# Down products of the first FFN block by Strassen's scheme, for the second to fifth group of features

## The chip, the cores and the metric

The kernel runs on one core of one Trainium2 chip. The metric is the device time of one execution in microseconds (us). Engines are called as in the profile: PE is TensorE's matmul, PEld its weight load, DVE VectorE, ACT ScalarE, POOL GpSimd, SP SyncE, which issues the DMAs.

## The reference, cut to what matters

One layer over 2112 tokens (2048 of a prompt, 64 of a running stream), float32, model width 1024. The change lies in the last part, the SwiGLU FFN with 22 x 128 = 2816 hidden features:

```python
D_FF = -(-8 * D_MODEL // (3 * 256)) * 256
...
    x = x + jnp.concatenate([o_delta, o_pool], axis=-1) @ w_out
    h = rmsnorm(x, norm2_w)
    x = x + (jax.nn.silu(h @ w_gate) * (h @ w_up)) @ w_down
...
    y_prompt = rmsnorm(hp, normf_w)
```

## The kernel before, in words

The mixer (projection, gated delta rule, pooling, output projection) fills the first 940 us and is not touched. The FFN then runs over three blocks `b` of 704 tokens, each cut into two halves of 352 columns. All activations lie with features on the 128 partitions and tokens along the free dimension.

Every product is taken in three matmuls on split operands: an operand is rounded on ACT (the high part), and DVE subtracts that from the original (the low part); high x high, high x low and low x high are added in PSUM. "A split" below is this pair, one cast on ACT and one subtraction on DVE.

`gate_up(b, f)` makes one feature tile `f` of 128 features (0 to 21). It joins gate and up, two halves of the inner dimension and two halves of the tokens into a 2 x 2 product of blocks, by the Strassen-Winograd scheme: seven products of 12 matmuls (`px`, `py`, `pz` in the trace), 84 for a feature. Its weights are seven matrices: 11, 22 and 12 are raw parts, S1 to S4 are sums that POOL forms. In block 0 they are all formed and split here (four loads, four POOL operations `wrS`, seven splits `ws` and `wsS`), and S1 to S4 are stored in DRAM split; blocks 1 and 2 load those four back and split only three. The hidden value is `raw` (`hr` in the trace), 128 x 704.

The down product adds groups of features into eight output tiles `ys` (`y`), which stay in SBUF. The groups are FGROUPS = 4, 4, 4, 4, 2, 4 features, `gi` 0 to 5; the prediction calls them group one to six. There are two forms.

`down` (plain): for each of eight output tiles a weight tile is loaded, split (`wsd`) and multiplied; each half of each tile has its own PSUM sum (`d`), which DVE adds into `y`. The hidden features are split half by half into the tiles `h3`.

`down_strassen`: pairs of features and pairs of output tiles are again a 2 x 2 product of blocks. `prep_down` loads two raw tiles (`wrdt`, `wrdl`), POOL forms four combinations (`wrda`, `wrdb`), and four tiles are split (`wsd11`, `wsdS3`, `wsdS2`, `wsd22`). `factors` makes seven matrices of a pair of features: four combinations on POOL (`q` and `hr`), seven splits (`hq`, `h7`). Seven products go to three PSUM sums (`dx`, `dy`, `dz`), of which DVE takes 28 adds into `y` for a group of four.

In block 0 all six groups are plain (`SDOWN = (1, 2)` names the blocks that use the scheme), and the six-slot ring `h3t` holds the split features. In blocks 1 and 2 the groups go by the scheme, but for the very last one. `h3t`, the pairs made by `factors` and the plain pairs `two` share the tag `op`, which has two buffers: a pair's tile comes free when the down that reads it is done.

The list `order` puts `gate_up` of all features in a row and each group's down behind the first feature of the next group; for `gi` 0 it is one feature later (`LATER = 1`):

```python
order += [("dn", b, gi) for gi, (f0, G) in enumerate(groups) if f == min(f0 + G + LATER * (gi == 0), NF - 1)]
```

From it comes `plan`, the order in which weights are prepared, up to `AHEAD` = 3 entries before use. The raw tiles have four buffers and three (`wraw`, `wraw2`), the split ones four and four (`wsp`, `wsp2`); one feature takes seven split tiles, one step of a scheme down four. The helper `Machine` records all operations and writes each engine's instructions in an order of its own, by cost rules and ranks (`issue`, `pick`); PSUM evictions get a higher rank (`hurry`). Because it writes them all, every instruction has one line in the profile (L280), and groups are told apart by tile names. `stats2(1)`, which prepares block 1's input (`xd`, `xt`), runs in block 0 beside the first two groups; the queues are static, so each engine works strictly in the written order.

Of the kernel before, what the change touches and what calls it, by code (L numbers as in the profile page):

```python
# [25 lines left out]
NF = 22  # L26
# [18 lines left out]
SUBS2 = ((0, N2), (N2, N2))  # L45
FGROUPS = (4, 4, 4, 4, 2, 4)

SDOWN = (1, 2)
LASTPOOLS = {3: ((0,), (1,), (2, 3))}

FW = ("11", "S1", "S2", "12", "S3", "S4", "22")
# [310 lines left out]
def hybrid_kernel(ctx, tc, a, o):  # L362
# [11 lines left out]
    def mm(out, lhsT, rhs, start, stop, **kw):  # L374
        nc.tensor.matmul(out, lhsT, rhs, start=start, stop=stop, **kw)
        n = 1
        for d in out.shape[1:]:
            n *= d
        cost(n, rhs.dtype)
# [39 lines left out]
    def pump():  # L419
        for c in list(chains):  # L420
            if c.runnable() and c.at <= clock["pe"]:
                c.step()
# [80 lines left out]
    groups, f0 = [], 0  # L503
# [4 lines left out]
    def halves(b, gi):  # L508

        return ((0,), (1,)) if (b, gi) == (NB2 - 1, len(groups) - 1) else ((0, 1),)  # L510

    def plain(b, gi):
        return b not in SDOWN or len(halves(b, gi)) > 1

    order = []
    for b in range(NB2):
        for f in range(NF):
            order.append(("gu", b, f))
            order += [("dn", b, gi) for gi, (f0, G) in enumerate(groups) if f == min(f0 + G + LATER * (gi == 0), NF - 1)]
    for op in order:  # L520
        if op[0] == "gu":
            plan.append(("gu", op[2]))
        else:
            plan += [("dn", m, *groups[op[2]]) for m in range(KT)] * len(halves(*op[1:])) if plain(*op[1:]) else [
                ("ds", m, *groups[op[2]]) for m in range(KT // 2 * groups[op[2]][1] // 4)]
# [131 lines left out]
    def weights(*key):  # L657
        weights_ahead()
        k, hl = ready.pop(0)
        assert k == key, (k, key)  # L660
        return hl
# [21 lines left out]
    def split(dst, sl, src):  # L683
        nc.scalar.copy(dst[:, 0, sl], src)
        tt(dst[:, 1, sl], src, dst[:, 0, sl].bitcast(F32), ALU.subtract)
# [742 lines left out]
    def load_h(b, names):  # L1428
        for nm in names:
            for k in range(4):  # L1430
                t = hq[nm][k]
                if "pool" in wq:
                    raw = wq["pool"].tile([P, N2], F32, tag="t", name=f"xh{nm}{k}_{b}", bufs=TB)
                else:
                    raw = wpool.tile([P, 512], F32, tag="xs", name=f"xh{nm}{k}_{b}", bufs=XBUFS["xs"])[:, :N2]
                nc.sync.dma_start(out=raw, in_=hpd[b, FH.index(nm), k])
                nc.scalar.copy(t[:, 0], raw)
                (nc.gpsimd if b and k in HPOOL else nc.vector).tensor_tensor(
                    out=t[:, 1], in0=raw, in1=t[:, 0].bitcast(F32), op=ALU.subtract)
                yield LAT_LOAD  # L1440
# [80 lines left out]
    def tmp(nm):  # L1521
        return f2.tile([P, N2], F32, tag="t", name=nm, bufs=TB)

    def hurry(what, *args):

        machine.boost = HURRY
        what(*args)
        machine.boost = 0

    def gate_up(b, f):  # L1530
        w = weights("gu", f)
        tag = f"{b}_{f}"
        raw = f2.tile([P, 2, N2], F32, tag="hr", name=f"hr{tag}", bufs=3)

        def add(ps, nw, nh, first=False):

            for i, t in enumerate(hq[nh]):
                ks = slice(i * P, (i + 1) * P)
                for q, (wi, ai) in enumerate(((0, 0), (0, 1), (1, 0))):
                    mm(ps, w[nw][:, wi, ks], t[:, ai, :], start=first and i == q == 0, stop=i == 3 and q == 2,  # L1540
                       skip_group_check=not first)
                pump()

        def sigmoid(e, x):
            act(e, x, AF.Exp, scale=-1.0)
            act(e, e, AF.Ln, bias=onec)
            act(e, e, AF.Exp, scale=-1.0)

        def finish(i, g, u):
            e = raw[:, i]  # L1550
            tt(e, e, g, ALU.mult)
            tt(e, e, u, ALU.mult)
            if b not in SDOWN:
                split(h3t[f % 6], slice(i * N2, (i + 1) * N2), e)


        x, y, z = (psg(f"p{i}_{tag}")[:, :N2] for i in "xyz")
        add(x, "11", "11", True)
        hurry(nc.scalar.copy, g1 := tmp(f"g1_{tag}"), x)
        add(y, "S1", "T1", True)  # L1560
        hurry(nc.scalar.copy, u2 := tmp(f"u2_{tag}"), y)
        add(x, "S2", "T2")
        hurry(nc.scalar.copy, g2 := tmp(f"g2_{tag}"), x)
        add(z, "12", "21", True)
        hurry(tt, g1, z, g1, ALU.add)
        sigmoid(raw[:, 0], g1)
        add(x, "S3", "T3")
        hurry(tt, u2, x, u2, ALU.add)
        add(y, "S4", "22")
        hurry(tt, g2, y, g2, ALU.add)  # L1570
        sigmoid(raw[:, 1], g2)
        finish(1, g2, u2)
        add(x, "22", "T4")
        finish(0, g1, x)
        return raw if b in SDOWN else h3t[f % 6]

    def down(b, gi, h3, ys, which, done):
        f0, G = groups[gi]
# [9 lines left out]
    def factors(b, f, u, v):  # L1588

        t = opool.tile([P, 13, N2], F32R, tag="op", name=f"hq{b}_{f}", bufs=2)  # L1590
        low = f2.tile([P, N2], F32R, tag="h7", name=f"h7{b}_{f}", bufs=2)
        t = {nm: (t[:, 2 * i], t[:, 2 * i + 1] if i < 6 else low) for i, nm in enumerate(FH)}

        def split(nm, x):
            hi, lo = t[nm]
            nc.scalar.copy(hi, x)
            tt(lo, x, hi.bitcast(F32), ALU.subtract)

        gt = (nc.vector if f == NF - 1 else nc.gpsimd).tensor_tensor
        t3, t2, t4 = (tmp(f"q{i}{b}_{f}") for i in (3, 2, 4))  # L1600
        for nm, x in (("11", u[:, 0]), ("21", v[:, 0]), ("22", v[:, 1])):
            split(nm, x)
        gt(out=t3, in0=v[:, 1], in1=u[:, 1], op=ALU.subtract)
        gt(out=u[:, 1], in0=u[:, 1], in1=u[:, 0], op=ALU.subtract)
        gt(out=t2, in0=v[:, 1], in1=u[:, 1], op=ALU.subtract)
        gt(out=t4, in0=v[:, 0], in1=t2, op=ALU.subtract)
        for nm, x in (("T1", u[:, 1]), ("T2", t2), ("T3", t3), ("T4", t4)):
            split(nm, x)
        return t
# [23 lines left out]
    six = [opool.tile([P, 3, 2, TB2], F32R, tag="op", name=f"h3_{i}", bufs=2) for i in range(2)]  # L1633
    h3t = [six[i // 3][:, i % 3] for i in range(6)]
    h3, ys = {}, {}

    def between(b):

        if b >= 0:
            yield from final_norm(b, ys.pop(b))  # L1640
        ys[b + 1] = new_y(b + 1)
        if b + 2 < NB2:
            yield from stats2(b + 2, f2, "t", TB)

    for op in order:
        b = op[1]
        if op[0] == "gu":
            f = op[2]
            if f == 0:
                fill.finish()  # L1650
            if op == ("gu", 0, 2):
                nxt = Chain(between(-1))
            h3[f] = gate_up(b, f)
            if b in SDOWN:
                gi = max(g for g, (f0, G) in enumerate(groups) if f0 <= f)
                if plain(b, gi):
                    if f == groups[gi][0] or f == groups[gi][0] + 2:
                        two = opool.tile([P, 2, 2, TB2], F32R, tag="op", name=f"h3l{f}", bufs=2)
                    for i in range(2):
                        split(two[:, f % 2], slice(i * N2, (i + 1) * N2), h3[f][:, i])  # L1660
                    h3[f] = two[:, f % 2]
                elif f % 2:
                    machine.boost = HURRY if f == NF - 1 else 0
                    h3[f] = factors(b, f, h3.pop(f - 1), h3[f])
                    machine.boost = 0
            if f == NF - 1 and b + 1 < NB2:
                nxt.finish()
                fill = Chain(load_h(b + 1, FH))
        else:
            f0, G = groups[op[2]]  # L1670
            while b not in ys:
                nxt.step()
            hs = [h3.pop(f0 + i) for i in range(G) if f0 + i in h3]
            if not plain(b, op[2]):
                down_strassen(b, op[2], hs, ys[b])
            for which in halves(b, op[2]) if plain(b, op[2]) else ():
                done = []
                if which != (0, 1):
                    Chain(last_norm(b, ys[b], *which, done))
                down(b, op[2], hs, ys[b], which, done)  # L1680
            if op[2] == len(groups) - 1 and b + 1 < NB2:
                nxt = Chain(between(b))
# [24 lines left out]
LATER = 1  # L1707
# [125 lines left out]
```

## Time and profile before

| | |
|---|---|
| three runs, median (lowest to highest) | 2320.13 us (2318.85 to 2321.16) |
| the profiled execution, own time | 2319.95 us |
| its span, first to last instruction | 2318.1 us |
| busy: PE, DVE, ACT, POOL | 99%, 73%, 58%, 36% |
| granted TensorE clock, mean | 0.999 |
| FFN block 0, by PE's rows | 940 to 1407 us |

The busy shares are averages over stages. How the engines stand to each other in block 0 is read from the windows by cycle, one cycle being four gate/up features and one down. An engine's busy time in a window counts overlapping instructions once, while the mean of a group is the duration of each.

### The profile page before, as it was taken

The numbers are of one execution on the slowest core, as the hardware profiler recorded it, in microseconds if no ns is written. First come the engines' busy times: TensorE is split into PE (matmuls) and PEld (weight loads), VectorE is DVE, ScalarE is ACT, GpSimd is POOL, SyncE is SP. The second block draws the span as 40 slices with busy tenths as digits, with TensorE's granted clock in tenths as the row PEclk, the third lists the DMA queues.
The fourth block names the chain that finished last, engine by engine and source line by source line (L and its number), as shares of the span: only waits on it lengthen the run. The fifth ranks groups of instructions, "written<-read, shape, count | busy, mean of one in ns | idle before, by whom it ended". The sixth has DMA issues, their size and how long they took to land.

```text
span 2318.1 us, 41343 instructions
## 1 busy us (share of the span) xinstructions
PE 2290.5 (99%) x14614; PEld 2143.5 (92%) x14614; DVE 1685.2 (73%) x3085; ACT 1352.2 (58%) x3004; POOL 834.4 (36%) x943
## 2 busy tenths in 40 slices
PE   8999999999999999999999999999999999999998
PEld 8898898878777878999999999999999999999998
DVE  8988755673677786787657675877877878767776
ACT  6887855683768864565445465554454574454444
POOL 4424222440234350554412144643331654331312
PEclk9999999999999999999999999999999999999999
DMA  8755375545465568867645377768645586455463
GB/s 294 255 179 177 140 259 198 186 147 199 164 209 172 157 207 283 301 240 261 220 157 192 136 243 230 244 214 277 195 138 191 175 299 216 149 189 187 149 198 104
DMA packets 218751, 471.34 MB, mean 203 GB/s; under 512 B 27056, under 2 KB 85424, under 8 KB 218544
## 3 DMA queue, kind: packets, MB, share of 16 engines
q1 hardware_dynamic: 218544, 468.71, 60.0%
q8 instruction: 115, 1.88, 0.3%
q14 instruction: 92, 0.75, 0.1%
HBM read 354.81 MB, written 113.80 MB: 202 GB/s over the span
## 4 chain that ended last, share of the span: by engine, by line
PE 88%; DVE 6%; ACT 3%; DMA 1%; issue 1%; POOL 0%; SPq 0%; POOLq 0%; DVEq 0%; ACTq 0%
PE px L280 21%; PE pp L280 16%; PE pz L280 13%; PE py L280 10%; PE d L280 8%; PE dx L280 6%; PE dy L280 3%; PE pk_p L280 2%; PE pt_p L280 2%; PE dz L280 2%; PE gr_p L280 1%; DVE y L280 1%; PE py_p L280 1%; ACT E L280 1%; DVE Yqk L280 1%
## 5 line engine op out<-in xcount | busy, mean ns | idle before, releaser
L280 PE MATMUL pp<-h,wsp 128*128 128x512 f32 (+1 forms) x2480 | 558.3, 366 | 10.1 <-DVE wsp L280 9.3
L280 PEld LDWEIGHTS pp<-h,wsp 128*128 128x128 f32 x2480 | 400.6, 190 | 56.3 <-ACT wsp L280 8.7
L280 ACT CAST ws<-wr 128x512 fp32r<-128x512 f32 x198 | 122.0, 618 | 197.8 <-PE px L280 55.8
L280 DVE TENSOR_TENSOR ws<-wr,ws 128x512 fp32r<-128x512 f32 x198 | 167.0, 845 | 49.8 <-ACT ws L280 45.7
L280 PE MATMUL d<-h,wsd 128*128 128x352 f32 x1056 | 170.1, 322 | 0.0
L280 PEld LDWEIGHTS d<-h,wsd 128*128 128x128 f32 x1056 | 168.8, 188 | 0.0
L280 PE MATMUL pz<-op,wsp 128*128 128x288 f32 (+1 forms) x768 | 160.6, 352 | 0.0
L280 ACT ACTIVATE hr<-g 128x352 f32<-128x352 f32 x132 | 65.7, 498 | 135.6 <-DVE g L280 135.2
L280 PE MATMUL px<-hA,ws 128*128 128x352 f32 x792 | 143.7, 322 | 0.0
L280 PE MATMUL py<-hB,wsS 128*128 128x352 f32 x792 | 142.6, 322 | 0.0
L280 PE MATMUL pz<-hB,ws 128*128 128x352 f32 x792 | 142.1, 322 | 0.0
L280 POOL TENSOR_TENSOR wrS<-wr,wrS 128x512 f32<-128x512 f32 x44 | 63.1, 1434 | 215.5 <-DMA wrS<-in_wu_dram 117.4
L280 PE MATMUL py<-hA,wsS 128*128 128x352 f32 x792 | 140.4, 322 | 0.0
L280 ACT CAST TV_p<-pt_p 128x512 f16<-128x512 f32 x192 | 111.1, 586 | 47.9 <-PE pt_p L280 46.7
L280 PE MATMUL px<-hA,wsS 128*128 128x352 f32 x792 | 138.2, 322 | 0.5 <-ACT g L280 0.5
L280 PE MATMUL px<-hBT,ws 128*128 128x352 f32 x792 | 138.2, 323 | 0.2 <-DVE u L280 0.2
L280 PE MATMUL px<-hBT,wsS 128*128 128x352 f32 x792 | 137.7, 322 | 0.0
L280 PEld LDWEIGHTS pz<-op,wsp 128*128 128x128 f32 x768 | 121.2, 188 | 12.3
L280 PEld LDWEIGHTS px<-hA,wsS 128*128 128x128 f32 x792 | 128.7, 188 | 1.2 <-ACT g L280 1.1
L280 PEld LDWEIGHTS px<-hA,ws 128*128 128x128 f32 x792 | 129.8, 188 | 0.1
L280 PEld LDWEIGHTS py<-hB,wsS 128*128 128x128 f32 x792 | 129.6, 188 | 0.0
L280 PEld LDWEIGHTS pz<-hB,ws 128*128 128x128 f32 x792 | 129.5, 188 | 0.0
(689 smaller groups left out, 5589.4 us busy)
## 6 DMA issues: line engine op xcount, KB each, us to landing
wsS<-gS SPq DMA_DIRECT2D x176, 512.0 KB, 4.5
wsp<-wnd SPq DMA_DIRECT2D x126, 512.0 KB, 3.3
gS<-wsS SPq DMA_DIRECT2D x88, 512.0 KB, 4.4
wr<-in_wg_dram SPq DMA_DIRECT2D x132, 256.0 KB, 3.1
wnd<-wsp SPq DMA_DIRECT2D x42, 512.0 KB, 5.0
xd<-x2d SPq DMA_DIRECT2D x96, 176.0 KB, 3.3
wr<-in_wu_dram SPq DMA_DIRECT2D x66, 256.0 KB, 3.5
wrd<-in_wd_dram SPq DMA_DIRECT2D x56, 256.0 KB, 3.3
```

The costliest lines, as they stand in the source:

```text
L280: getattr(getattr(self.nc, op.eng), name)(*args, **kw)
```

## The change

`STR0 = (1, 2, 3, 4)` takes the place of `SDOWN`: in block 0 the groups two to five use `down_strassen` and `factors`; group one stays plain with the ring `h3t`, and group six is plain, with its features split into `two` as in the last group of block 2. `LATE0 = (1, 2)`: in block 0 the downs of groups two and three stand one feature later in `order`.

```diff
-SDOWN = (1, 2)
+STR0 = (1, 2, 3, 4)
+LATE0 = (1, 2)
...
     def plain(b, gi):
-        return b not in SDOWN or len(halves(b, gi)) > 1
+        return (b == 0 and gi not in STR0) or len(halves(b, gi)) > 1
...
-            order += [("dn", b, gi) for gi, (f0, G) in enumerate(groups) if f == min(f0 + G + LATER * (gi == 0), NF - 1)]
+            order += [("dn", b, gi) for gi, (f0, G) in enumerate(groups) if f == min(f0 + G + LATER * (gi == 0 or b == 0 and gi in LATE0), NF - 1)]
...
     def gate_up(b, f):
...
+        gi = max(g for g, (f0, G) in enumerate(groups) if f0 <= f)
+        six = b == 0 and gi < min(STR0)
...
-            if b not in SDOWN:
+            if six:
                 split(h3t[f % 6], slice(i * N2, (i + 1) * N2), e)
...
-        return raw if b in SDOWN else h3t[f % 6]
+        return h3t[f % 6] if six else raw
...
-            if b in SDOWN:
-                gi = max(g for g, (f0, G) in enumerate(groups) if f0 <= f)
+            gi = max(g for g, (f0, G) in enumerate(groups) if f0 <= f)
+            if b or gi >= min(STR0):
                 if plain(b, gi):
```

All engines' orders are the same up to feature 5 of block 0. On PE, before, group two's plain down (`d0_1_...`: block 0, `gi` 1, output tile, half) starts in the eighth feature (`px_0_8`, `py_0_8`):

```order
L280 MATMUL py_0_8_3223<-hB22_2908,wsS4_141_3190 128x352 x2
L280 MATMUL px_0_8_3222<-hBT3_2907,wsS3_141_3189 128x352 x12
L280 MATMUL py_0_8_3223<-hB22_2908,wsS4_141_3190 128x352 x10
L280 MATMUL d0_1_0_0_3230<-h3_1_2967,wsd_142_3199 128x352 x3
L280 MATMUL px_0_8_3222<-hBT4_2909,ws22_141_3191 128x352 x12
L280 MATMUL d0_1_0_0_3230<-h3_1_2967,wsd_142_3199 128x352 x3
L280 MATMUL d0_1_0_0_3230<-h3_0_2966,wsd_142_3199 128x352 x6
```

On PE, in the changed kernel, the same group's products (`dx0_1_0`, `dy0_1_0`, `dz0_1_0`: first pair of output tiles) start in feature 9 and read the pairs of features 4, 5 and 6, 7 (`hq0_5`, `hq0_7`):

```order
L281 MATMUL px_0_9_3271<-hBT3_2907,wsS3_142_3214 128x352 x12
L281 MATMUL py_0_9_3272<-hB22_2908,wsS4_142_3215 128x352 x6
L281 MATMUL dx0_1_0_3290<-hq0_5_3107,wsd11_143_3231 128x352 x3
L281 MATMUL dx0_1_0_3290<-hq0_7_3242,wsd11_143_3231 128x352 x3
L281 MATMUL px_0_9_3271<-hBT4_2909,ws22_142_3216 128x352 x12
L281 MATMUL dy0_1_0_3291<-hq0_5_3107,wsdS3_143_3232 128x352 x3
L281 MATMUL dy0_1_0_3291<-hq0_7_3242,wsdS3_143_3232 128x352 x3
L281 MATMUL dz0_1_0_3292<-hq0_5_3107,wsd11_143_3231 128x352 x3
L281 MATMUL dz0_1_0_3292<-hq0_7_3242,wsd11_143_3231 128x352 x3
L281 MATMUL dx0_1_0_3290<-hq0_5_3107,wsdS2_143_3233 128x352 x3
```

The plain sums, 12 matmuls for each half of an output tile, have become short runs of six on three sums, and the down has moved behind feature 9.

On DVE, before, around the last add of group two (`y7` from `d0_1_7`); 150 and 151 are the weights of features 9 and 10:

```order
L280 TENSOR_TENSOR wsS1_151_3272<-wrS1_151_3265,wsS1_151_3272 128x512
L280 TENSOR_TENSOR y7_0_3037<-y7_0_3037,d0_1_7_0_3294 128x352
L280 TENSOR_TENSOR y7_0_3037<-y7_0_3037,d0_1_7_1_3295 128x352
L280 TENSOR_TENSOR ws22_150_3261<-wr22_150_3250,ws22_150_3261 128x512
L280 TENSOR_TENSOR ws11_151_3271<-wr11_151_3264,ws11_151_3271 128x512
L280 TENSOR_TENSOR ws12_151_3274<-wr12_151_3267,ws12_151_3274 128x512
L280 TENSOR_TENSOR wsS2_151_3273<-wrS2_151_3269,wsS2_151_3273 128x512
L280 TENSOR_TENSOR g1_0_9_3314<-pz_0_9_3313,g1_0_9_3314 128x352
```

On DVE, in the changed kernel, around the last add of the same group; 147 is the weights of feature 10, the next one on PE, and `hq0_9`, `h70_9` are the factors of features 8 and 9:

```order
L281 TENSOR_TENSOR ws12_147_3303<-wr12_147_3296,ws12_147_3303 128x512
L281 TENSOR_TENSOR ws22_147_3306<-wr22_147_3295,ws22_147_3306 128x512
L281 TENSOR_TENSOR y7_0_3037<-y7_0_3037,dx0_1_3_3341 128x352
L281 TENSOR_TENSOR hq0_9_3277<-hr0_8_3255,hq0_9_3277 128x352
L281 TENSOR_TENSOR hq0_9_3277<-hr0_9_3270,hq0_9_3277 128x352 x2
L281 TENSOR_TENSOR hq0_9_3277<-hr0_8_3255,hq0_9_3277 128x352
L281 TENSOR_TENSOR hq0_9_3277<-q20_9_3280,hq0_9_3277 128x352
L281 TENSOR_TENSOR hq0_9_3277<-q30_9_3279,hq0_9_3277 128x352
L281 TENSOR_TENSOR h70_9_3278<-q40_9_3281,hq0_9_3277 128x352
L281 TENSOR_TENSOR wsS4_147_3305<-wrS4_147_3299,wsS4_147_3305 128x512
L281 TENSOR_TENSOR g1_0_10_3362<-pz_0_10_3361,g1_0_10_3362 128x352
```

Before, the splits that follow the group's last add belong mostly to the feature after next; now the seven feature splits of a pair follow it, and behind them one weight split of the next feature.

## The prediction

> **What bounds the kernel now.** I read the page first: busy time by engine, the slices, then the granted clock.
>
> ```profile
> span 2318.1 us, 41343 instructions
> PE 2290.5 (99%) x14614; PEld 2143.5 (92%) x14614; DVE 1685.2 (73%) x3085; ACT 1352.2 (58%) x3004; POOL 834.4 (36%) x943
> PEclk9999999999999999999999999999999999999999
> ```
>
> TensorE (PE) is busy for 99% of the span at the full clock. So work taken off PE counts in full, as long as the others keep up. Whether they do in the first FFN block must be read there. The windows show two cycles of that block (four gate/up features and one down each; columns: stretch, its length, busy us with counts for PE, PEld, DVE, ACT, POOL, then clock, DMA share, GB/s), and below them cycles of the second and third block, which use Strassen's scheme for the down products already:
>
> ```profile
> 1094.00:1178.00 84.00, 84.00 (x527) 84.00 (x526) 60.31 (x93) 39.92 (x79) 29.28 (x22) 1.00 0.60 212
> 1178.00:1263.00 85.00, 85.00 (x533) 85.00 (x532) 54.14 (x88) 41.63 (x82) 22.22 (x16) 1.00 0.48 176
> 1560.00:1640.00 80.00, 80.00 (x501) 80.00 (x500) 64.99 (x107) 37.91 (x77) 36.35 (x37) 1.00 0.74 245
> 1640.00:1721.00 81.00, 81.00 (x508) 80.91 (x507) 60.17 (x105) 38.78 (x79) 27.09 (x28) 1.00 0.57 183
> 1870.00:1951.00 81.00, 81.00 (x506) 80.75 (x505) 68.11 (x110) 50.66 (x108) 44.09 (x42) 1.00 0.72 242
> ```
>
> PE has no gap in any of them. VectorE (DVE) stands at 57 of 84.5 us in the first block, and reaches 68 of 81 in a later one without PE losing anything. What PE waited for (in total, times, longest), first in the first block, 940 to 1410 us, then in the blocks that use the scheme, 1410 to 2276 us:
>
> ```profile
> PE px L280 <- ACT g L280: 0.5, 1, 0.5
> ...
> PE dy L280 <- DVE y L280: 0.8, 1, 0.8
> PE dy L280 <- DVE hq L280: 0.7, 1, 0.7
> PE dz L280 <- DVE y L280: 0.6, 2, 0.3
> PE dy L280 <- ACT hq L280: 0.6, 1, 0.6
> PE px L280 <- DVE u L280: 0.2, 1, 0.2
> ```
>
> So the scheme has cost 2.9 us of waits in two whole blocks, eleven groups.
>
> **What is removed: matmuls.** A plain down of four features is 8 output tiles x 2 halves x 4 features x 3 terms = 192 matmuls; by the scheme it is 7 products x 4 pairs of tiles x 2 pairs of features x 3 = 168. For the group of two it is 96 against 84. Three groups of four and the one of two change: 3 x 24 + 12 = 84 matmuls fewer. Their price, from the chain in order of time (start, length, line):
>
> ```profile
> 1320.19 15.38 PE d L280 x96
> ...
> 1503.66 1.93 PE dx L280 x12
> ...
> 1778.80 2.50 DVE y L280 x6
> ```
>
> 15.38 / 96 = 0.160 us for the plain form, 1.93 / 12 = 0.161 for the other; both have 352 columns, so neither is dearer. So 84 x 0.1602 = 13.46 us come off PE. A cycle then is 504 matmuls, 80.7 us.
>
> **What is added: work beside PE.** The groups of DVE in the two cycles 1094 to 1263 us (mean ns last before the bar):
>
> ```profile
> L280 DVE TENSOR_TENSOR wsS<-wrS,wsS 128x512 fp32r<-128x512 f32 x32 | 24.9, 787 | 10.3 <-ACT wsS L280 10.0
> L280 DVE TENSOR_TENSOR y<-y,d 128x352 f32<-128x352 f32 x32 | 16.5, 517 | 18.2 <-PE d L280 18.2
> L280 DVE TENSOR_TENSOR wsd<-wrd,wsd 128x512 fp32r<-128x512 f32 x16 | 13.2, 833 | 3.3 <-ACT wsd L280 3.1
> L280 DVE TENSOR_TENSOR hr<-hr,g 128x352 f32<-128x352 f32 x16 | 13.1, 817 | 4.7 <-ACT hr L280 4.7
> L280 DVE TENSOR_TENSOR h<-hr,h 128x352 fp32r<-128x352 f32 x16 | 12.0, 758 | 0.7 <-ACT h L280 0.6
> ```
>
> and of two cycles with the scheme, 1560 to 1721 us:
>
> ```profile
> L280 DVE TENSOR_TENSOR y<-y,dx 128x352 f32<-128x352 f32 x32 | 15.9, 510 | 3.7 <-PE dx L280 3.5
> L280 DVE TENSOR_TENSOR hq<-hr,hq 128x352 fp32r<-128x352 f32 x16 | 12.9, 810 | 0.0
> L280 DVE TENSOR_TENSOR y<-y,dy 128x352 f32<-128x352 f32 x16 | 8.2, 510 | 0.4 <-PE dy L280 0.3
> L280 DVE TENSOR_TENSOR wsdS<-wrdb,wsdS 128x512 fp32r<-128x512 f32 x8 | 8.0, 998 | 0.0
> L280 DVE TENSOR_TENSOR wsd<-wrdt,wsd 128x512 fp32r<-128x512 f32 x8 | 7.4, 930 | 0.1
> L280 DVE TENSOR_TENSOR hq<-q,hq 128x352 fp32r<-128x352 f32 x8 | 6.8, 878 | 0.0
> L280 DVE TENSOR_TENSOR wsdS<-wrda,wsdS 128x512 fp32r<-128x512 f32 x8 | 6.5, 810 | 0.3 <-DMA wsS<-gS 0.2 <-ACT wsdS L280 0.2
> L280 DVE TENSOR_TENSOR wsd<-wrdl,wsd 128x256 fp32r<-128x256 f32 x8 | 6.2, 772 | 0.0
> L280 DVE TENSOR_TENSOR y<-y,dz 128x352 f32<-128x352 f32 x8 | 4.1, 508 | 0.0
> L280 DVE TENSOR_TENSOR h<-q,hq 128x352 fp32r<-128x352 f32 x4 | 2.6, 651 | 0.0
> ```
>
> A cycle is half of each row. Adds into y: 28 for 16, (15.9 + 8.2 + 4.1) / 2 = 14.1 for 8.3, so +5.8. Down weights: 16 splits for 8, (8.0 + 7.4 + 6.5 + 6.2) / 2 = 14.1 for 6.6, so +7.5. Features: 14 splits for 8, (12.9 + 6.8 + 2.6) / 2 = 11.2 for 6.0, so +5.2.
>
> 18.5 us by durations. Instructions in a row overlap: six adds took 2.50 us, 0.42 each for a duration of 0.51, so the 26 added ones may occupy 2.4 us less: 16 to 18.5. DVE comes from 57 to 73 to 76 of 80.7 us, 91 to 94%, more than any cycle of the trace shows. The difference from the later blocks is that gate/up weights are split from raw here, 28 splits a cycle, while those load stored parts.
>
> ACT casts for the same 14 added splits; even at DVE's 12.7 us for them it comes from 40 to 42 us only to 55 of 80.7, and stays the cover. The down weights are the same bytes, four pairs of raw loads for eight single ones; moved one feature later, those of groups two and three fall on SP's queue behind the four loads and four stores of one more feature. At a DMA share of 0.48 to 0.60 in these cycles I cost that at nothing; with a full queue it would be a load's 3.3 us to landing (last column), once a group, 12 us in all:
>
> ```profile
> wrd<-in_wd_dram SPq DMA_DIRECT2D x56, 256.0 KB, 3.3
> ```
>
> POOL gets new work, priced by two rows of those cycles:
>
> ```profile
> L280 POOL TENSOR_TENSOR q<-hr,hr 128x352 f32<-128x352 f32 x8 | 9.1, 1139 | 42.2 <-DVE hr L280 39.3 <-ACT wsd L280 2.6
> L280 POOL TENSOR_TENSOR wrdb<-wrdt,wrdb 128x256 f32<-128x256 f32 x9 | 8.6, 953 | 0.5
> ```
>
> Sixteen combinations of down weights at 0.95 and eight of features at 1.14 make 24 us; POOL comes from 26 to 50 of 80.7. It works in order: behind the feature combinations, which wait for the second feature of a pair, stand weights that PE needs at least one feature (13.5 us) later, so nothing is late by that alone.
>
> **Stalls.** Three terms, each small. What the scheme costs where it runs now: 2.9 us x 3.5 / 11 groups = 0.9.
> The lead of the weights: in the order before, the last add of group two has all but one of feature 9's seven weight splits ahead of it, and feature 10's follow at once. Now seven feature splits come behind that group's last add (their slot is free only then), and behind them the S4 split of the very next feature, which PE reads after four products, 4 x 1.93 = 7.7 us. Seven splits take 3.6 us at 0.52 and 6.1 at the means above, behind the casts of ACT. Loss 0 to 1 for each of the two late groups; I take 1.0 together.
> From feature 13 to 18 two downs fall into five features: 185 DVE instructions in the order (60 adds at 0.51, 61 splits of 512 at 0.80, 9 of 256 at 0.77, 20 feature splits at 0.81, 10 products of two SBUF operands at 0.82, 25 other at 0.52) make 124 us by durations and 107 with 0.09 of overlap each, while PE has 5 x 13.46 + 2 x 26.9 = 121. Loss 0 to 3; I take 1.1.
>
> Together 3.0. From feature 18 on a plain group follows, and the queue drains; what is late there is hidden again. Blocks two and three keep their order, and the end only shifts.
>
> **Sum.** The profiled execution took 2319.95 us (span 2318.1). 2319.95 - 13.46 + 3.0 = 2309.5; the median of the runs is 0.2 above it: 2309.7.
>
> **Rivals.** *The cover holds entirely:* stalls as in the block before, at most 1 us: 2307. For it speaks that single slices of the later blocks had DVE near full without a gap; against it, 91 to 94% sustained.
>
> *DVE is held up by POOL and becomes the bound (slower).* Splits of one shape vary in the trace (min/median/max ns):
>
> ```profile
> L280 DVE TENSOR_TENSOR wsS<-wrS,wsS x88: 675/693/1836, 934.1 to 1361.7; 128x512 fp32r<-128x512 f32 x88
> L280 DVE TENSOR_TENSOR hq<-hr,hq x80: 507/520/1274, 1422.6 to 2214.2; 128x352 fp32r<-128x352 f32 x80
> ```
>
> In 1560 to 1721 us the rows above exceed these medians by 13.3 us (8 x (0.305 + 0.237 + 0.117) = 5.3 in the weights, 16 x 0.29 + 8 x 0.358 + 4 x 0.131 = 8.0 in the features), with 63.4 us of POOL: 0.21 us of delay for each us of POOL. With 50 us of POOL a cycle that is 10.5 us, about what the means above already hold; without it DVE has some 64. PE begins to wait at a rate of (80.7 - 64) / 50 = 0.33; the change turns slower beyond 0.2% from (13.46 + 4.64) / 3.5 = 5.2 us a cycle on, a rate of 0.44. At 0.5 the loss is (64 + 25 - 80.7) x 3.5 = 29 us, and the time 2335.5. Against it: the stretch 1870 to 1951 had 44 us of POOL and 68 of DVE.
> The Trainium skill (SBUF — State Buffer, Who interferes with whom) says that a DVE instruction with two SBUF inputs and a GpSimd one that reads SBUF exclude each other, the later one blocked for the whole of the other. The maxima agree: 1836 is a median plus 1.1 us, near a whole POOL instruction. By that rule, as an estimate, 66 such DVE operations a cycle (28 + 16 + 14 splits, 8 products) that each meet POOL at its busy share of 0.62 and wait half an instruction, 0.55 us, lose 22.5 us a cycle; DVE comes to 86.5, and the time to about 2327. The measured means show half of that delay.
>
> *The gain is eaten up (no change):* DVE in its order, with stalls of 9 to 18 us: 2320. For it speaks only the shorter lead of the weights at every one of the four groups, 2.5 to 5 us each; nothing in the trace shows one stall over 0.8.
>
> **How the numbers follow.** About 0.2% (4.6 us) is what a measurement of this kernel can tell from no change. Forecast, with stalls of 1 to 8 us: 0.72. Cover entire: 0.14. No change: 0.05. Slower: 0.09. Faster is the first two, 0.86. The range runs from no stall at all, 2306.5, to a stall of 8, 2314.7: 0.86 lies in it, and its upper part is needed for the unknown lead of the weights.
>
> **What would show it.** Right: 84 matmuls fewer, `d` rows with half the count, `dx`, `dy`, `dz` rows grown, PE still without gaps in 1030 to 1100 us, DVE at 73 to 76 in an 81 us cycle, small waits of PE for DVE near the ends of groups two and three and around features 16 to 18. Wrong: PE waits of several us for `ws` or `wsS` after a down, DVE at 98% and more over a whole cycle, means of 512-wide splits above 1.1 us, or PE waiting for POOL's combinations or for DMA.

## The result, and the profile after

Measured: 2324.27 us (median of 22 runs, 2320.66 to 2327.64) against 2320.8 us for the kernel before beside it (22 runs, 2318.85 to 2324.13). The ratio is 1.0015, with a 95% interval of 1.0009 to 1.0020: slower by 0.15%, less than the 0.2% that the prediction drew as its line. Forecast were 2309.7 us, range 2306.5 to 2314.7. The profiled execution of the changed kernel took 2327.14 us, 2.9 above its median; the trace below is that of a run on the long side.

The page of the kernel before, chain of waits by engine:

```profile
PE 88%; DVE 6%; ACT 3%; DMA 1%; issue 1%; POOL 0%; SPq 0%; POOLq 0%; DVEq 0%; ACTq 0%
```

The page of the changed kernel, busy time and the same chain:

```profile
span 2325.3 us, 41424 instructions
PE 2283.5 (98%) x14530; PEld 2130.9 (92%) x14530; DVE 1763.3 (76%) x3178; ACT 1367.7 (59%) x3049; POOL 926.5 (40%) x1027
...
PE 77%; DVE 13%; ACT 3%; DMA 3%; issue 3%; POOL 0%; SPq 0%; DVEq 0%; POOLq 0%; ACTq 0%
```

The 84 matmuls are gone (14614 to 14530), yet the span grew by 7.2 us, and DVE's part in the chain doubled. The windows of the changed kernel show where (columns as in the prediction: length, busy us with counts for PE, PEld, DVE, ACT, POOL, clock, DMA share, GB/s); first four cycles of the first block, then three short stretches:

```profile
1030.00:1111.00 81.00, 79.12 (x489) 77.84 (x488) 72.35 (x100) 41.70 (x84) 53.57 (x42) 1.00 0.71 243
1111.00:1192.00 81.00, 79.43 (x491) 78.22 (x489) 74.59 (x113) 43.38 (x89) 50.07 (x43) 1.00 0.59 205
1192.00:1273.00 81.00, 77.69 (x480) 76.90 (x481) 77.50 (x116) 43.21 (x89) 48.88 (x43) 1.00 0.44 150
1273.00:1354.00 81.00, 75.47 (x454) 73.92 (x453) 73.20 (x118) 35.37 (x71) 38.13 (x30) 0.98 0.42 147
1100.00:1120.00 20.00, 20.00 (x125) 19.66 (x124) 19.97 (x33) 8.89 (x17) 15.11 (x16) 1.00 0.54 172
1120.00:1140.00 20.00, 19.16 (x118) 18.53 (x117) 20.00 (x34) 6.58 (x13) 12.54 (x11) 1.00 0.42 137
1320.00:1340.00 20.00, 16.82 (x92) 15.94 (x92) 19.05 (x35) 6.12 (x11) 6.86 (x5) 0.91 0.21 67
```

DVE at 72 to 77.5 of 81 us and, in the first three cycles, POOL at about 50 are what was forecast. PE is not full beside them: it stands for 1.9, 1.6, 3.3 and 5.5 us. Note the fifth row: DVE full, POOL three quarters busy, and PE without a gap. The waits of PE in the first block, in total, times, longest (before: one of 0.5):

```profile
PE px L281 <- DVE u L281: 4.7, 5, 1.4
PE px L281 <- ACT g L281: 3.4, 3, 1.7
PE dx L281 <- DVE y L281: 3.4, 3, 2.1
PE dz L281 <- DVE hr L281: 0.6, 1, 0.6
PE pz L281 <- ACT ws L281: 0.5, 1, 0.5
PE py L281 <- ACT wsS L281: 0.4, 1, 0.4
PE d L281 <- ACT h3l L281: 0.2, 1, 0.2
```

PE waits for PSUM tiles to be emptied (`u`, `g`, `y`), hardly for a weight. From its first matmul to the first of block 1 the first block took 471.7 us, before 466.0 (0.6 us for four matmuls of block 1's norm are taken off both). At 0.1602 us for each of its 2820 matmuls (before 2904) it would take 451.8 (465.2), so 19.9 us are lost, before 0.8. This "loss" is the measure of what follows. Gaps hold 17.5 of the 19.9, if a gap is where one matmul starts over 0.12 us later after the last than 0.160; the waits above, counted from the ends of the matmuls, add up to 13.2. The rest of the program took 1.5 us longer.

One wait followed back. The timeline of the changed kernel (start, length), DVE:

```profile
1235.20 0.69 DVE L281 TENSOR_TENSOR wsS<-wrS,wsS 128x512 fp32r<-128x512 f32 x1
...
1236.40 1.61 DVE L281 TENSOR_TENSOR hr<-hr,g 128x352 f32<-128x352 f32 x1
1238.05 1.64 DVE L281 TENSOR_TENSOR hr<-hr,u 128x352 f32<-128x352 f32 x1
1239.62 1.78 DVE L281 TENSOR_TENSOR ws<-wr,ws 128x512 fp32r<-128x512 f32 x1
1241.32 1.60 DVE L281 TENSOR_TENSOR hr<-hr,g 128x352 f32<-128x352 f32 x1
1242.96 0.52 DVE L281 TENSOR_TENSOR hr<-hr,px 128x352 f32<-128x352 f32 x1
```

POOL, ACT and PE in the same stretch:

```profile
1235.93 1.71 POOL L281 TENSOR_TENSOR wrS<-wr,wrS 128x512 f32<-128x512 f32 x1 [7.02 <-DVE wsS L281]
1238.02 2.83 POOL L281 TENSOR_TENSOR wrS<-wrS,wr 128x512 f32<-128x512 f32 x2 [0.39 <-DVE hr L281]
1241.08 1.46 POOL L281 TENSOR_TENSOR wrS<-wr,wrS 128x512 f32<-128x512 f32 x1 [0.23 <-DMA wr<-in_wg_dram]
1243.51 0.48 ACT L281 CAST hq<-hr 128x352 fp32r<-128x352 f32 x1 [4.33 <-DVE hr L281]
1243.90 0.44 ACT L281 COPY g<-px 128x352 f32<-128x352 f32 x1
1244.40 0.91 PE L281 MATMUL px<-hBT,wsS 128*128 128x352 f32 x4 [1.68 <-ACT g L281]
```

While POOL forms four sums one behind the other, four DVE operations take 1.61, 1.64, 1.78 and 1.60 us. Without POOL beside it a split of the same size (first line) takes 0.69, and a product with one operand in PSUM (last line) 0.52. DVE is over 4 us late; ACT's cast of the new feature waits 4.33 us for it; behind the cast in ACT's order stands the copy that empties `px`; and PE stands for 1.68 us. The wait is booked on ACT, but it comes from a run of DVE operations that each lasted about as long as one of POOL's. POOL in turn had stood for 7.02 us before its first sum, until a split on DVE (`wsS`) was done; by the kernel's text such a split frees a raw tile of the second set, into which POOL writes. So the two engines wait for each other.

All of DVE's subtractions, sums and products in the first block bear this out. With two operands in SBUF and 512 columns, 96 of them lay beside no POOL instruction and took 0.68 us in the mean, 0.70 at most; 113 overlapped one, and took 1.13 in the mean and 1.83 at most. With 352 columns it is 0.52 (53) against 1.04 (80). With one operand in PSUM it is 0.51 with POOL beside it or not (135 and 96). How much of the loss this makes is what the runs must tell.

A second part is the clock. The windows of the changed kernel around the longest gap:

```profile
1327.00:1331.00 4.00, 1.86 (x12) 1.58 (x11) 4.00 (x6) 1.14 (x2) 2.17 (x2) 1.00 0.01 2
1331.00:1335.00 4.00, 4.00 (x18) 4.00 (x17) 3.21 (x7) 0.00 (x0) 0.00 (x0) 0.57 0.21 66
1335.00:1339.00 4.00, 4.00 (x27) 4.00 (x27) 3.98 (x9) 1.86 (x3) 0.00 (x0) 1.00 0.21 45
```

PE had stood for 2.1 us at a stretch; then the granted clock was 0.5 for 3.41 us. Eleven matmuls began 0.29 us apart for 0.16, so 1.5 us of the 17.5 in gaps are this.

### The profile page after: what moved, and what is told of

Same layout as the page of the kernel before. It is cut to its first block, busy times and chain, and to the rows that moved or that the text cites. A ratio compares the mean times of both kernels' runs of the same rounds, so it can differ in the third digit from the quotient of the medians.

```text
span 2325.3 us, 41424 instructions
## 1 busy us (share of the span) xinstructions
PE 2283.5 (98%) x14530; PEld 2130.9 (92%) x14530; DVE 1763.3 (76%) x3178; ACT 1367.7 (59%) x3049; POOL 926.5 (40%) x1027
## 4 chain that ended last, share of the span: by engine, by line
PE 77%; DVE 13%; ACT 3%; DMA 3%; issue 3%; POOL 0%; SPq 0%; DVEq 0%; POOLq 0%; ACTq 0%
PE px L281 17%; PE pp L281 16%; PE pz L281 12%; PE py L281 8%; PE dx L281 7%; PE d L281 3%; PE dy L281 3%; DVE y L281 2%; PE pk_p L281 2%; PE dz L281 2%; PE pt_p L281 2%; DVE hr L281 1%; PE gr_p L281 1%; DMA gS<-wsS 1%; DVE hq L281 1%
## 5 line engine op out<-in xcount | busy, mean ns | idle before, releaser
L281 PE MATMUL pp<-h,wsp 128*128 128x512 f32 (+1 forms) x2480 | 557.7, 365 | 11.5 <-DVE wsp L281 10.8
L281 DVE TENSOR_TENSOR ws<-wr,ws 128x512 fp32r<-128x512 f32 x198 | 176.2, 892 | 36.4 <-ACT ws L281 32.3
L281 POOL TENSOR_TENSOR q<-hr,hr 128x352 f32<-128x352 f32 x52 | 59.4, 1143 | 239.1 <-DVE hr L281 233.8
L281 PE MATMUL px<-hBT,ws 128*128 128x352 f32 x792 | 138.8, 323 | 5.8 <-DVE u L281 5.8
L281 DVE TENSOR_TENSOR y<-y,dx 128x352 f32<-128x352 f32 x240 | 119.7, 513 | 23.7 <-PE dx L281 22.5
L281 PEld LDWEIGHTS px<-hBT,ws 128*128 128x128 f32 x792 | 128.2, 188 | 8.4 <-DVE u L281 7.9
L281 PEld LDWEIGHTS px<-hBT,wsS 128*128 128x128 f32 x792 | 128.7, 188 | 2.0 <-ACT g L281 2.0
```

The lines of the kernel that those rows point to most:

```text
L281: getattr(getattr(self.nc, op.eng), name)(*args, **kw)
```

## The experiments

Two theories first. L: DVE's queue is too long; at over 90% any disturbance reaches PE, whatever POOL does. P: POOL does it, by its own time in the chain (sums of weights, combinations) or by holding up DVE's reads ("the port"). The expectations call P by POOL's own time or its buffers Q, the late downs as the cause O, and the group of two features F. All times are medians beside runs of the kernel before on the same chip. The runs were made in four sets on different chips, where the kernel before had 2320.3 to 2321.5 us, so times of two rows compare to about 1 us. DVE and POOL are busy us in the 325 us from 1017 to 1342, by the windows of one profiled run; loss is worked out as above, from the same run. The profiled runs lay between 2.5 us below (e16) and 3.6 above (e15) their medians, so losses less than about 3 us apart say little.

The helper `Machine` plans by cost rules, so an edit also changes the order in which the other operations are written. Of some 604 DVE instructions of the first block, e8 keeps at most 417 in the changed kernel's order, e2 478 and e13 484. Each run thus measures its edit together with a new order. That any new order would move the loss as far is unlikely: e3 and e12 keep at most 455 and 439, and each lost 19.8 us as against 19.9.

| kernel | us | ratio to before, 95% | DVE | POOL | loss |
|---|---|---|---|---|---|
| before | 2320.8 | | 226.9 | 102.5 | 0.8 |
| changed | 2324.27 | 1.0015, 1.0009 to 1.0020 | 297.8 | 191.5 | 19.9 |
| e1_nolow | 2319.59 | 0.9989, 0.9980 to 0.9998 | 267.9 | 186.6 | 11.3 |
| e2_nocomb | 2312.31 | 0.9960, 0.9948 to 0.9973 | 290.1 | 138.8 | 3.9 |
| e3_notlate | 2327.09 | 1.0020, 1.0011 to 1.0029 | 296.2 | 187.2 | 19.8 |
| e4_no4 | 2321.77 | 1.0004, 0.9995 to 1.0013 | 294.0 | 179.9 | 12.0 |
| e5_dveload | 2326.03 | 1.0017, 1.0008 to 1.0026 | 279.1 | 102.2 | 5.1 |
| e6_poolload | 2322.22 | 1.0005, 0.9997 to 1.0014 | 235.1 | 171.9 | 2.4 |
| e7_fill | 2323.03 | 1.0006, 0.9998 to 1.0015 | 286.6 | 180.2 | 15.7 |
| e8_psum | 2317.81 | 0.9981, 0.9972 to 0.9990 | 299.7 | 186.8 | 11.6 |
| e9_psum_no4 | 2315.63 | 0.9981, 0.9972 to 0.9989 | 285.3 | 176.7 | 7.7 |
| e10_before_psum | 2319.94 | 0.9997, 0.9988 to 1.0006 | 218.1 | 101.7 | 0.5 |
| e11_load | 2318.51 | 0.9991, 0.9982 to 0.9999 | 287.6 | 138.9 | 10.6 |
| e13_fill1 | 2315.56 | 0.9977, 0.9968 to 0.9986 | 289.7 | 151.9 | 7.9 |
| e14_xs3_raw4 | 2342.48 | 1.0090, 1.0076 to 1.0104 | 296.6 | 193.1 | 26.3 |
| e15_xs3 | 2337.00 | 1.0071, 1.0058 to 1.0083 | 289.0 | 188.8 | 26.0 |
| e16_late3 | 2315.70 | 0.9979, 0.9969 to 0.9989 | 285.0 | 177.4 | 7.2 |

**Less for DVE, less for POOL.** In e1 block 0's scheme leaves out the low parts of the features' factors (DVE's subtractions), the high part standing in for them:

```diff
+            if b:
                 tt(lo, x, hi.bitcast(F32), ALU.subtract)
+            else:
+                t[nm] = (hi, hi)
```

> The changed kernel; left out: in block 0 the low parts of the factors (the seven DVE subtractions of each pair of features), the high part is multiplied in their place. PE, ACT and POOL keep their instructions; DVE loses 14 of them a cycle, some 11 us of 81. Theory L (DVE's queue is too full, and what PE waits for stands behind splits): the 17 us of gaps of PE in block 0 fall to under 4, the time to 2308 to 2312. Theory P (POOL stretches DVE's splits; the number of DVE instructions matters little): half of the gaps stay, 2316 to 2319. Theory O (the late downs and the short lead of the weights) and theory F (the group of two features): 2320 to 2324.

In e2 POOL's combinations of the down weights are left out in block 0, the raw tiles standing in for them:

```diff
+        if first:
+            s31, s24 = low, top
+        else:
             s31, s24 = (wtiles(f"d{i}", True)[0]() for i in "ab")
...
```

> The changed kernel; left out: in block 0 the sixteen POOL combinations of down weights of a group, the splits read the raw tiles in their place. PE, DVE and ACT keep their instructions; POOL loses 15 us a cycle. Theory P: DVE's splits get shorter by 0.1 us and more, the gaps fall to under 5 us, the time to 2309 to 2313. Theory L: DVE falls only from 94% to about 90%, 2315 to 2319. Theories O and F: 2320 to 2324.

30 us less on DVE took away 8.6 us of loss and 4.7 of time; 53 us less on POOL (and 8 on DVE) took away 16.0 and 12.0. The time of e1 lies in none of its ranges, that of e2 in P's. The windows of e2, and PE's waits in its first block:

```profile
1017.00:1342.00 325.00, 323.16 (x2010) 321.60 (x2010) 290.09 (x467) 174.60 (x354) 138.77 (x105) 1.00 0.58 199
...
PE px L281 <- ACT g L281: 1.2, 2, 0.8
PE pz L281 <- ACT ws L281: 0.5, 1, 0.5
PE py L281 <- ACT wsS L281: 0.4, 1, 0.4
```

DVE is at 89% here with PE nearly without gaps, and the time is 2312.3, near the forecast. DVE's load alone does not settle the loss: at 88 to 89% it was 3.9 (e2), 7.9 (e13), 10.6 (e11) and 15.7 (e7).

**The order.** e3 puts the two late downs back, e4 takes group five out of the scheme:

```diff
-LATE0 = (1, 2)
+LATE0 = ()
```

> The changed kernel with the downs of groups two and three at their plain place, not one feature later. Theory O: the lead of the weights comes back, the gaps behind these downs go, 2313 to 2320. Theory L: the same DVE work falls into a shorter stretch beside the preparation of block 1, slower than the changed kernel, 2325 to 2330. Theory F: unchanged, 2323 to 2326.

```diff
-STR0 = (1, 2, 3, 4)
+STR0 = (1, 2, 3)
```

> The changed kernel with group five (two features) plain: 12 matmuls, 1.9 us, are given back to PE. Theory F (its six sums of three matmuls each starve PE): the 6.7 us of gaps between features 17 and 20, the halved clock among them, go; 2318 to 2320.5. Theory L: DVE is as full up to there, half of those gaps stay, 2321 to 2324. Theory O: 2325 to 2327.

The later downs are not the cause: without them the loss is the same and the median 2.8 us higher, as theory L had it. Group five saves 12 matmuls, 1.9 us. Without it the loss in the profile is 7.9 us smaller, but the rest of that execution was 3.3 longer, and by the medians the kernel gains 2.5 us. That is the range of theory L, not of F. So group five does not pay, and costs 2.5 us net.

**Load added to the kernel before.** e5 adds subtractions of two SBUF operands on DVE behind the adds of groups two to five, 32 for a group of four and 16 for the group of two; e6 adds 24 and 16 on POOL. Their results are not used; e5 has

```diff
+            if b == 0 and 1 <= gi <= 4:
+                for i in range(4 if G == 4 else 2):
+                    tt(tmp(f"x{i}_{gi}_{m}"), ys[m][:, i % 2], ys[m][:, i % 2], ALU.subtract)
```

> The kernel before (plain downs in block 0) with idle work for DVE: at groups two to five of block 0, 32 subtractions of two SBUF operands of 352 columns for a group of four (16 for the one of two) into a scratch tile that nobody reads, some 17 us a cycle, as much as the change adds. POOL as before. Theory L (DVE's queue alone): PE gets gaps of 10 us and more, 2330 to 2338. Theory P (POOL and DVE together): gaps of 0 to 4 us, 2320.5 to 2325.

> The kernel before with idle work for POOL: at groups two to five of block 0, 24 (16) subtractions of two SBUF operands of 352 columns into a scratch tile, some 26 us a cycle, as much as the change adds. DVE's instructions as before, 57 us a cycle and some 6 more by POOL. Theory P taken as POOL alone: 2330 and more. Theory P taken as both together (DVE has the slack to be held up): gaps of 0 to 4 us, 2320.5 to 2325. Theory L: the same, 2321 to 2322.

The windows of e5, then those of e6:

```profile
1017.00:1342.00 325.00, 323.11 (x2015) 321.92 (x2014) 279.06 (x468) 148.78 (x293) 102.17 (x72) 1.00 0.54 188
```

```profile
1017.00:1342.00 325.00, 324.09 (x2025) 323.54 (x2025) 235.12 (x367) 148.76 (x295) 171.86 (x157) 1.00 0.54 190
```

52 us more on DVE cost 4.3 us of loss and 5.2 of time, between the ranges of P and L; 69 more on POOL cost 1.6 and 1.4, in the range of P taken as both together. The change adds 71 and 89, and costs 19.1. By these slopes, added up, it would have cost 5.9 + 2.1 = 8. So the loads taken one by one do not explain it: with both, the loss is over twice the sum. The comparison has a weak side: the added operations stand in other places than the scheme's, and nothing waits for their results.

**The port.** e7 replaces each of POOL's combinations in block 0 by three fills of the same part of the tile, which read nothing (the scheme's down weights there are without meaning):

```diff
+        if first:
+            for o in (left(s31), right(s31), left(s24), right(s24)):
+                for i in range(3):
+                    nc.gpsimd.memset(o, 0.01)
```

> The changed kernel; in block 0 each of POOL's sixteen combinations of down weights is replaced by three fills of the same tile with a constant, which read nothing; the sums are left out. POOL stays as busy in time or nearly, the chain raw tile, POOL, split stays, only POOL's reads go. Theory P by the shared read port: like the kernel without combinations, 2311 to 2315. Theory Q (POOL's queue is late, or the buffers): like the changed kernel, 2321 to 2325.

e8 keeps all of the change, and leaves the two sums `z + g1` and `y + g2` of each feature in PSUM, so that the products after them have one operand in SBUF:

```diff
-        hurry(tt, g1, z, g1, ALU.add)
-        sigmoid(raw[:, 0], g1)
+        hurry(tt, z, z, g1, ALU.add)
+        sigmoid(raw[:, 0], z)
...
-        finish(0, g1, x)
+        finish(0, z, x)
```

> The changed kernel with two sums of each feature (z + g1, y + g2) written back into PSUM in place of SBUF, so that the two products hr x g have one SBUF operand each and need no shared port. Nothing is left out. Theory P: these products fall from 0.87 to 0.52 us, 2.8 us of DVE a cycle that stood right ahead of what PE waits for; gaps fall by 4 to 10 us, 2314 to 2320. Theory Q: 2322 to 2326. If PSUM's banks are short for it, slower than 2326.

e10 does the same to the kernel before:

> The kernel before (plain downs in block 0) with the sums z + g1 and y + g2 kept in PSUM. If that edit gains only by taking gaps away: 2320 to 2321.5, no change, since block 0 had 0.8 us of gaps before. If it is worth something by itself in all three blocks: 2316 to 2319.

The groups of DVE in 1100 to 1261 us, in the changed kernel and then in e8 (count, busy us, mean ns):

```profile
L281 DVE TENSOR_TENSOR hr<-hr,g 128x352 f32<-128x352 f32 x16 | 12.4, 773 | 1.1 <-ACT hr L281 1.0
L281 DVE TENSOR_TENSOR hr<-hr,u 128x352 f32<-128x352 f32 x8 | 6.2, 780 | 0.2
```

```profile
L281 DVE TENSOR_TENSOR hr<-hr,u 128x352 f32<-128x352 f32 x8 | 6.9, 863 | 0.2
L281 DVE TENSOR_TENSOR hr<-hr,pz 128x352 f32<-128x352 f32 x9 | 4.6, 511 | 1.9 <-ACT hr L281 1.9
L281 DVE TENSOR_TENSOR hr<-hr,py 128x352 f32<-128x352 f32 x8 | 4.1, 510 | 0.2 <-ACT hr L281 0.2
```

With an operand in PSUM the product takes 0.51 us beside the same POOL work, the other one (`hr<-hr,u`) 0.86, in the changed kernel 0.78. The loss falls by 8.3 us and the time by 6.5 (2324.27 to 2317.81), though DVE's busy time is the same (299.7 for 297.8). So DVE's total did not decide it; that it was the lateness of two operations close to PE's evictions is the likely reading, but e8's new order is in it too. In the kernel before, which has no loss to give back, the same edit does nothing that can be measured. e7, on the other hand, gained only 1.2 us, about 4 of loss; POOL's reads of the combinations are not the main thing about them. (e7's clock stood at 0.5 for 6.83 us in the first block, some 3 us of its loss.) Nor did the fills hold DVE up in e7: 26 operations with two operands in SBUF and 512 columns that overlapped fills alone took 0.68 us in the mean and 0.69 at most, as without POOL; 90 that overlapped a POOL operation which reads took 1.21.

**POOL's time, its tiles, its loads.** e11 fills the two tiles by loads and not by POOL (7.3 MB more are read); e13 by one short fill for each half (`range(1)` in e7's edit). In both the scheme's down weights of block 0 are without meaning.

```diff
+            for t, m0 in ((s31, m * M), (s24, m * M + KT // 2)):
+                nc.sync.dma_start(out=parts(t), in_=a["wd"][...])
```

> The changed kernel; in block 0 POOL's sixteen combinations of down weights are replaced by loads into the same two tiles (raw weights, not the sums, which are left out), so tiles, buffers, ACT and DVE stay and only POOL's step goes, for 4 MB more of DMA. If POOL's own queue and its reads are the cause: like the kernel without combinations, 2311 to 2314. If the second raw buffers (three of them) are the cause: 2320 to 2325. If DMA gets in the way: over 2325.

> Each pair of POOL's combinations in block 0 is replaced by a single short fill of the same tiles (about 0.3 us in place of about 2 us), so the values of the scheme's down weights are left out. The tiles, their buffers, and who waits for whom are as in the fill run before; POOL falls to about 155 of 325 us. If POOL's time in the chain was what is left after the reads are gone, PE's gaps in block 0 fall to 3 to 5 us and the time to 2312 to 2315. If it is the tiles that the combinations keep (raw buffers of the second set, loads that start later), it stays at 2316 to 2320 with 7 to 10 us of gaps, near the version that loads the combinations (2318.5).

The windows of e7, and then of e13:

```profile
1017.00:1342.00 325.00, 315.96 (x1934) 311.44 (x1933) 286.62 (x453) 167.98 (x339) 180.21 (x269) 0.99 0.55 189
```

```profile
1017.00:1342.00 325.00, 321.69 (x1989) 318.24 (x1988) 289.70 (x462) 173.08 (x348) 151.90 (x160) 1.00 0.57 196
```

The edits differ in nothing but the number of POOL's fills: same tiles, nothing read by them; the written order is another (at most 489 of 604 DVE instructions keep theirs). 28 us less of POOL take 7.8 us of loss away, 3 of them at half clock, and 7.5 us of time (7.0 against the kernel before beside each), with DVE as busy as before. So POOL's own time is a cause, without the port's reads. From e13 to e2, where the two tiles and the waits around them are gone as well, come another 4.0 of loss and 3.2 of time. Both e11 and e13 came out between the ranges of their two forecasts, so POOL's time is not all that is left.

**Raw buffers.** POOL's combinations hold the raw tiles of the second set longer, which has three buffers. A first attempt, e12_raw4, paid for a fourth with scratch tiles, and made PE wait 7.2 us for `g`: 2332.4 us, 1.0052 (1.0040 to 1.0065), which tells nothing on the raw tiles.

> The changed kernel with four buffers in place of three for the second set of raw weight tiles, where POOL writes its sums, and six for seven of the small scratch tiles to make room. If POOL is held by these buffers: gaps fall by 5 us and more, 2314 to 2320. If not: 2322 to 2326.

e14 pays with a buffer of `xs`, and e15 takes that buffer away alone:

```diff
-XBUFS = {"xs": 4, "xc": 3}
+XBUFS = {"xs": 3, "xc": 3}
...
-        return (lambda: pool.tile([P, 512], F32, tag="wraw" + x, name=f"wr{nm}_{at}", bufs=3 if second else 4),
+        return (lambda: pool.tile([P, 512], F32, tag="wraw" + x, name=f"wr{nm}_{at}", bufs=4 if second else 4),
```

> The second set of raw tiles has four buffers for three, paid for with one of four buffers of xs, a tile of the norm. To be read against e15_xs3. If three raw buffers cause part of the waits (a load starts late, so a cast and a split are late), block 0's gaps fall by 4 to 8 us against e15_xs3, and so does the time. If POOL and DVE are late by their own work, the two runs agree within 1.5 us.

> The changed kernel with three buffers of xs for four and nothing else: the control for e14_xs3_raw4. Expected within 3 us of the changed kernel (2321 to 2327), with gaps of 14 to 20 us in block 0; the tile is used beside the first two groups only, so a loss would lie there.

The control missed its own range: the missing `xs` buffer costs 12.7 us; in the trace the first block starts 9.1 us later and takes 6.1 longer. Against it the fourth raw buffer changes the loss from 26.0 to 26.3, and the median is 5.5 us higher, which neither forecast had. So the pair gives no sign that a fourth buffer helps, in a kernel that has other waits besides. It does not clear the buffers either: in the wait followed above POOL's 7.02 us ended with the split that frees such a tile.

**A better version.** e9 joins e8 and e4, e16 puts the down of group four one feature later as well (`LATE0 = (1, 2, 3)`):

> Candidate: the changed kernel with both edits, the sums z + g1 and y + g2 kept in PSUM, and group five (two features) plain. 12 matmuls, 1.9 us, come back; of the 9.5 us of gaps that the kernel with sums in PSUM had in block 0, those behind feature 18 (5 us) should go. Theory P or Q alike: 2313 to 2316. If the gaps move to another place: 2317 to 2320.

> Sums in PSUM, groups two to four by the scheme, and the down of group four one feature later as well. If what is left of the gaps (6 us) comes from the early down of group four, which falls five features' work of DVE into four, the time goes to 2312 to 2314. If lateness only moves the same work, it stays at 2315 to 2317.

Both beat both kernels: 2315.6 and 2315.7 us, 0.2% below the kernel before and 8.6 below the changed one. By e16 the early down of group four is not what is left. Of the 11.5 us that 72 matmuls are worth, 5 arrive.

## Why the prediction was wrong

**Right: the matmuls, and every load.** 84 fewer. DVE was forecast at 73 to 76 us of 80.7 in a cycle; the four windows have 74.4 of 81 in the mean. POOL was forecast at 50 and stood at 49 to 54 in the first three. PE waited only 0.9 us for weights, so that they come early enough was right as well.

**The step that failed: the term Stalls, 3.0 us.** Measured are 16.9: the 13.46 that PE no longer has to do, and the 3.47 by which the median is higher. In the trace the first block alone lost 19.1 us more than before. In place of 3.0 us the trace shows loss around every down that changed, counted from the first matmul of a feature to that of the next: 4.7 us in feature 9 (group two's down), 1.8 in 13 (group three's), 4.6 in 15 and 16 (group four's), 7.1 in 18 and 19 (group five's, 1.5 of it at half clock). 11.5 us of PE's waits are for PSUM tiles, and the runs tie the loss to DVE and POOL together. All three parts of the term went wrong:

- *What the scheme costs where it runs now, 0.9.* 2.9 us in eleven groups were carried over by count. Those blocks had DVE at 60 to 68 of 81 us and POOL at 27 to 44; here they are at 74 and about 50. e5, e6 and the changed kernel show that the loss goes neither by count nor by the sum of the loads, and is larger once both are high. Even both loads do not settle it: e7 and e16 have almost the same (287 and 180 us, 285 and 177) and lose 15.7 and 7.2.
- *The lead of the weights, 1.0.* It was priced as a wait of PE for a split, for each of the two late groups. The features of these two downs lost 6.5 us, but PE waited only 0.9 us for weights in all, and e3, without the late groups, has the same loss.
- *Features 13 to 18, 1.1.* DVE's work was set against PE's as two sums, with a loss only where DVE's is larger. But the windows lose 1.9, 1.6, 3.3 and 5.5 us where DVE is at 72 to 78 of 81; features 13 to 17 lost 6.6. After them come the features in which "the queue drains; what is late there is hidden again": 18 and 19 lost 7.1. The down of group five falls there, and e4, which leaves it out, is 2.5 us faster though it has 12 matmuls more.

**"Nothing is late by that alone", of POOL's order: wrong.** That PE needs those weights a feature later was checked for the weights only. e7 against e13 shows POOL's time costing some 7 us with tiles and reads alike. In the timeline above POOL's sums for the next features come in one go after 7 us of waiting for DVE, just where DVE's products are due, and lengthen them.

**The rivals.** "DVE is held up by POOL" had the right pair of engines. Its price of 0.21 us of delay for each us of POOL was too low: it counted only the splits of the down product's weights and features. Counted over all of DVE's subtractions, sums and products, as what they last beyond the 0.68, 0.52 and 0.42 us of an undisturbed one (512, 352 and 256 columns), the same stretch of the kernel before has 0.31. The changed kernel has 0.38 from 1017 to 1342 us (72.6 us by 191.7 of POOL), above the 0.33 from which the rival lets PE wait. But it wants DVE full on average, and DVE never was full over a cycle. By the Trainium skill's rule (SBUF — State Buffer, Who interferes with whom) the prediction estimated 22.5 us of delay a cycle, 86.5 us of DVE and 2327 us. The delay was near that, 18 to 20 us in each of the first three cycles, and single operations did last as long as the rule says (1.60 to 1.78 us in the timeline above). The cycle still measured 74.4, in part because the 64 us to which the delay was added held some of it already; the time came near 2327 by another road, which is luck. "The gain is eaten up", 9 to 18 us of stalls and 2320 us, was nearest by its stalls; it got 0.05, because no stall of over 0.8 us stood in the trace of before. That trace had no cycle with both engines this busy, so it could not have shown one.

**What is shown, what stays open.** Shown: load added to one engine alone, somewhat less than the change adds, costs at most 4.3 us of loss (5.2 of time); relieving DVE, or POOL, or only two products of each feature gives back 8 to 16 (4.7 to 12.0 of time); and DVE's operations with two operands in SBUF are lengthened by a POOL operation that reads, not by fills. Shown for one wait, and argued for the others: the path through a run of lengthened DVE operations, ACT's in-order queue and a PSUM tile. The parts do not add up to a split by cause: e1's 8.6, e8's 8.3 and e2's 16.0 are together more than the whole (1.5 us of e2's and of e8's is the stretch at half clock, which their first blocks do not have). Open is how much the new order of each run adds, and what e11's loads and its two tiles cost against e2 (6.7 us of loss; the windows there show DMA at 0.64 for 0.58).

## What to carry to other kernels

Moving work from the bounding engine to engines in strict order costs nothing only while one of them has slack: with two that wait for one another at 90% and 60%, a load sum that still fits says little, and the loss has to be bounded from a stretch that has both loads, or by a run. Look then at what stands just ahead of the evictions that the bounding engine waits for, and make those operations immune (here two sums left in PSUM gave 6.5 us) before shortening the total. Take the scheme where the gain for each added operation is largest, and leave out the pieces that save least: the group of two saved 1.9 us of matmuls, and the kernel is 2.5 us faster without it.

## What the runs showed of the hardware

A DVE operation with two operands in SBUF was held up by a POOL operation that reads SBUF, and not by one that only writes: with 512 columns 0.68 us without POOL, 1.13 beside its sums and combinations (changed kernel), 0.68 beside its fills (e7). With one operand in PSUM it was not held up, 0.51 us either way.

The granted clock fell to 0.5 after gaps that are short: in the changed kernel after 2.1 us without a matmul, with the 1.86 busy of 4 us shown above, for 3.41 us. In the first block it did so in e1, e11 and e12 for 3.41 us, in e7 for 6.83, in e3 for 6.83 and 3.41. In the 3.41 us before each of these PE was busy for 1.3 to 1.7; in e11 the longest of three waits there was 0.8 us. The Trainium skill (TensorE: Matmul & The Clock Gate, Part 1: The HAM clock gate) gives at least one idle window of about 3.4 us as the condition; the length of the slow stretch agrees with that window, while no gap before it was as long. A wait of 2 us on a tuned kernel can so cost 1.5 us more than itself.
